# Value projections of two attention branches by seven block products, and weight-block sums made by adding transfers

## The chip, the cores and the metric

The kernel runs on one core of a Trainium2 chip. The metric is the time of one execution on the device in microseconds (us), as a median over runs. The core's engines work side by side: TensorE (PE; its weight loads are listed as PEld), VectorE (DVE), ScalarE (ACT), GpSimd (POOL) and SyncE (SP), which issues the transfers. Each engine takes its instructions in the order of its own queue and waits on semaphores for the others.

## The reference

Two layers of a sequence encoder on an input of 512 rows and 1024 columns, all in float32. A layer projects its input x with one wide weight matrix (1024 x 9216) into the inputs of three branches: retention (four heads, values of 256), chunked attention (eight heads of 64, with a bias by relative position) and differential attention (four heads, each with two softmax maps, values of 128). The branch outputs are projected back to 1024 columns, scaled by sigmoid gates that also come from the projection, added, projected once more, added to x and normalised. A gated feed-forward network (hidden width 2816) and a second normalisation follow. In the core:

```python
h = jnp.einsum('bsd,de->bse', x, w_in[l])
rq, rk, rv, rg, cq, ck, cv, dq, dk, dv, gates = jnp.split(h, splits, axis=-1)
...
p = jax.nn.softmax(s, axis=-1).reshape(B, H, 2, Q_BLOCK, S)
p = p[:, :, 0] - lam * p[:, :, 1]
...
ffn = jnp.einsum('bsf,fd->bsd', jax.nn.silu(u_gate) * u_up, w_ffn_out[l])
```

The parts of `h` that matter here are `cv` and `dv` (512 columns each), the values of chunked and of differential attention, and `rv` and `rg` (1024 columns each), the values and the gate of retention.

## The kernel before

Every float32 operand of a matmul is carried as a pair of float32r tiles, a rounded part and the rest, so that one product of tiles is three matmuls (`mm3`, L121): high by high, high by low, low by high. Weights come from memory in 1 MB pieces into staging tiles `st` (NSTAGE = 3 of them, L49). ScalarE copies the high part into `wh`, VectorE subtracts to make `wl`. There are AHEAD = 3 buffers of each (L48). The work is a list of items (`run_items`, L485): an item is a set of weight pieces and a function that runs its matmuls; the pieces are requested up to three ahead. Between items, and at places within them, small pieces of work (`s_q`, `s_r1`, `s_c1`, `s_d0` and so on) are put in groups beside an item, so that TensorE has matmuls while VectorE and ScalarE do a softmax or a split. A planner lays out each engine's instructions, by the order of the program and the free buffers. Intermediate tiles of 128 x 512 share one pool of 61 slots (NSLOT, L47); gate tiles that are made early (EARLY, L45) are sent to memory and fetched back.

Some products of 512 x 1024 by 1024 x 1024 are not made from eight block products but from seven, with sums of blocks before and after (the Winograd form). `Halves` (L158) holds the weight side: blocks (0,0), (0,1), (1,0), (1,1) of 512 x 512, and four sums T1 to T4 of them. `Quarters` (L228) holds the activation side, whose sums `s_q` makes. `product` (L268) runs one of the seven, with 2 x 4 x 3 = 24 matmuls of 512 columns. This form is used for two groups of retention values and gates in each layer (`u_rvg`, L656: p and q) and for two groups of the output matrix of the feed-forward network (`fout_items`, L1149). VectorE makes the sums T1 to T4 in the staging tiles: `add` (L182), in two instructions each. One staging tile of its own, `sa`, carries (0,0), T1 and T2 through the group. `Staged` (L216) splits a block in two halves.

`cv` and `dv` are projected in the ordinary way by `u_vhl` (L776): for each of four row tiles 8 x 3 matmuls of 512 columns, 96 in all, with the split halves left in slots for the attention that follows. The item of `cv` carries the retention of heads 2 and 3 (`s_r1`, `s_r2`) beside it, the item of `dv` the last steps of chunked attention.

The order of the items is written out from L1021. In the stage before attention it is: first item, gate (0,1), p's m1, gate (0,2), p's y and x, gate (0,3), p's m2 and v, gate (2,0), p's g and h, an item of retention queries (`u_rqk`), q's m1, an item of retention keys, q's y, gate (2,1), q's x, m2, v, g, h, then `cv`. A gate or `u_rqk` item has 48 matmuls of 512 columns.

Of the kernel before, what the change touches and what calls it, by code (L numbers as in the profile page):

```python
# [17 lines left out]
P = 128  # L18
# [26 lines left out]
EARLY = [(0, 0), (0, 1), (0, 2), (0, 3), (2, 0), (2, 1)]  # L45
# [3 lines left out]
NSTAGE = 3  # L49
# [7 lines left out]
def trunk(ctx, tc, x_in, xT_in, w_in, ret_norm_g, da_norm_g, lq1, lk1, lq2, lk2, w_a, w_b, w_c, b_merge, w_out,  # L57
# [12 lines left out]
    make_identity(nc, ident)  # L70
    mhalf = cpool.tile([P, 4], F32, name="mhalf")
    nc.gpsimd.memset(mhalf, -0.5)
    saved = [dram.tile([S, D], F32, name=f"saved{i}") for i in range(2 * DEPTH - 1)]

# [83 lines left out]
    class Halves:  # L158
# [6 lines left out]
        def __init__(self, w, r0, kh, cols=(0, 512)):  # L165
            self.w, self.r0, self.kh, self.cols = w, r0, kh, cols

        def load(self, i, j, tag="st", **kw):
            t = wst.tile([P, 2048], F32, tag=tag, name=tag, **kw)[:, :512 * self.kh]
            t = t.rearrange("p (k c) -> p k c", k=self.kh)  # L170
            r = P * (self.r0 + i * self.kh)
            c = self.cols[j]
            nc.sync.dma_start(t, self.w[r:r + P * self.kh, c:c + 512].rearrange("(k p) c -> p k c", p=P))
            return t

        def parts(self):
            h = max(self.kh // 2, 1)
            return [slice(a, min(a + h, self.kh)) for a in range(0, self.kh, h)]

        def add(self, t, u):  # L180
            for s in self.parts():
                nc.vector.tensor_add(t[:, s], t[:, s], u[:, s])  # L182

        def block(self, t):
            return Staged(t, self.kh, self.parts())

        def b11(self):
            self.a = self.load(0, 0, "sa", bufs=1)
            return self.block(self.a)

        def t1(self):
            self.add(self.a, self.load(0, 1))
            return self.block(self.a)

        def t2(self):
            self.add(self.a, self.load(1, 1))
            return self.block(self.a)

        def b21(self):
            return self.block(self.load(1, 0))  # L200

        def b22(self):
            self.d = self.load(1, 1)
            return self.block(self.d)

        def t3(self):
            c = self.load(0, 1)
            self.add(c, self.__dict__.pop("d"))
            return self.block(c)

        def t4(self):
            b = self.load(1, 0)
            self.add(b, self.__dict__.pop("a"))
            return self.block(b)

    class Staged:  # L216


        def __init__(self, st, nk, parts):
            n = 512 * nk  # L220
            self.nk = nk
            self.hi = wsp.tile([P, 2048], F32R, tag="wh", name="wh")[:, :n].rearrange("p (k c) -> p k c", k=nk)
            self.lo = wsp.tile([P, 2048], F32R, tag="wl", name="wl")[:, :n].rearrange("p (k c) -> p k c", k=nk)
            for s in parts:
                nc.scalar.copy(self.hi[:, s], st[:, s])  # L225
                nc.vector.tensor_sub(self.lo[:, s], st[:, s], f(self.hi[:, s]))  # L226
# [167 lines left out]
    class Norm:  # L394
# [11 lines left out]
        def finish(self, t):  # L406
# [3 lines left out]
            rs = small.tile([P, 2], F32, tag="rs", name="rs")  # L410
            nc.vector.tensor_scalar_add(rs[:, 0:1], mv[:, 1:2], LN_EPS)  # L411
            nc.gpsimd.tensor_tensor(rs[:, 1:2], rs[:, 0:1], mhalf[:, 0:1], op=ALU.pow)
            for z, gam in zip(self.z[t], self.gam):
                nc.vector.scalar_tensor_tensor(z, z, mv[:, 0:1], gam, op0=ALU.subtract, op1=ALU.mult)  # L414
            for hf, (z, bet) in enumerate(zip(self.z[t], self.bet)):
                nc.vector.scalar_tensor_tensor(z, z, rs[:, 1:2], bet, op0=ALU.mult, op1=ALU.add)  # L416
                nc.sync.dma_start(self.dst[P * t:P * t + P, 512 * hf:512 * hf + 512], z)

        def normalise(self, t):
            mv = small.tile([P, 2], F32, tag="mv", name="mv")  # L420
            nc.vector.bn_aggr(mv, self.st[t])
            rs = small.tile([P, 2], F32, tag="rs", name="rs")
            nc.vector.tensor_scalar_add(rs[:, 0:1], mv[:, 1:2], LN_EPS)
# [887 lines left out]
```

## Time and profile before

| What | Value |
|---|---|
| Time, median of 3 runs | 1924.13 us (1923.47 to 1924.18) |
| The profiled execution | 1923.79 us |
| Its span, first to last instruction | 1922.0 us |
| Mean granted TensorE clock | 0.998 |
| Busy: PE, DVE, ACT, POOL | 99%, 68%, 46%, 2% |
| Matmuls | 9250 |
| Moved by DMA | 241 MB, mean 125 GB/s |
| Transfers issued by | SP alone (hardware queue 1: 239.5 MB, 39.2% of the 16 engines' time) |

The span is the profiled execution between its first and last instruction. Busy shares are unions of instruction times; they say how much an engine does, not whether something waits for it. Part 2 of the profile's page cuts the span into 40 slices of 48 us, in tenths.

### The profile page before, as it was taken

The page shows a single profiled execution, that of the slowest core. Times are in us where ns is not written, and L with a number is a line of the kernel's source. Part 1 is how long each engine was busy: PE and PEld are TensorE (multiplying, and loading weights), DVE is VectorE, ACT ScalarE, POOL GpSimd, SP SyncE. Part 2 cuts the span into 40 slices and gives each one's busy share as a digit, 9 for nine tenths or more (in the row PEclk, how much of TensorE's full clock was granted, in tenths as well). Part 3 has the DMA queues.
Part 4 walks back from the last instruction along what each step waited for, and adds up shares of the span by engine and source line. Part 5 has one row for each costly group of instructions (what it writes and reads, how often), then busy time and mean ns, then how long its engine had stood idle before and what let it go on. Part 6 is the DMA issues. An engine that isn't in the chain of part 4 may idle for free. (4 is left out here: it accounts for less than half of the span.)

```text
span 1922.0 us, 23998 instructions
## 1 busy us (share of the span) xinstructions
PE 1907.8 (99%) x9250; PEld 1606.2 (84%) x9250; DVE 1305.7 (68%) x2183; ACT 876.8 (46%) x1551; POOL 46.2 (2%) x73
## 2 busy tenths in 40 slices
PE   9999999999999999999999999999999999999998
PEld 7888888888888888888898888888888898888886
DVE  7677766667765757666588776665776667675666
ACT  5444455567634333333255544554765343333331
POOL 0000000000000000000000000000000000000000
PEclk9999999999999999999999999999999999999999
DMA  7453343233154444434335444332221624444331
GB/s 251 168 171 121 121 135 112 57 94 97 44 183 125 148 137 127 137 109 143 121 140 185 156 138 135 113 95 92 77 87 62 202 78 153 148 137 132 110 127 48
DMA packets 242070, 241.05 MB, mean 125 GB/s; under 512 B 8366, under 2 KB 180516, under 8 KB 241956
## 3 DMA queue, kind: packets, MB, share of 16 engines
q1 hardware_dynamic: 241956, 239.52, 39.2%
q8 instruction: 72, 1.18, 0.3%
q14 instruction: 42, 0.34, 0.1%
HBM read 224.77 MB, written 14.73 MB: 125 GB/s over the span
## 5 line engine op out<-in xcount | busy, mean ns | idle before, releaser
L122 PE MATMUL pt<-xTh,wh 128*128 128x512 f32 (+1 forms) x1584 | 596.8, 377 | 1.5 <-ACT xTh L519 1.5
L123 PE MATMUL pt<-xTl,wh 128*128 128x512 f32 (+1 forms) x1584 | 593.6, 375 | 1.1 <-DVE xTl L520 1.1
L124 PE MATMUL pt<-xTh,wl 128*128 128x512 f32 (+1 forms) x1584 | 593.2, 375 | 0.0
L151 ACT CAST wh<-st 128x1024 fp32r<-128x1024 f32 (+1 forms) x282 | 268.6, 981 | 272.3 <-issue 138.8
L152 DVE TENSOR_TENSOR wl<-st,wh 128x1024 fp32r<-128x1024 f32 (+1 forms) x282 | 314.0, 1137 | 106.8 <-ACT wh L151 106.3
L123 PEld LDWEIGHTS pt<-xTl,wh 128*128 128x128 f32 x1584 | 298.8, 189 | 54.0 <-DVE xTl L520 2.1
L122 PEld LDWEIGHTS pt<-xTh,wh 128*128 128x128 f32 x1584 | 298.3, 189 | 54.4 <-ACT xTh L519 2.3
L124 PEld LDWEIGHTS pt<-xTh,wl 128*128 128x128 f32 x1584 | 298.4, 188 | 53.6
L225 ACT CAST wh<-st 128x1024 fp32r<-128x1024 f32 x64 | 64.9, 1051 | 97.6 <-PE pt L123 65.0
L1105 DVE TENSOR_TENSOR fth<-fth,pt 128x512 f32<-128x512 f32 x44 | 30.2, 686 | 104.4 <-PE pt L124 104.4
L225 ACT CAST wh<-sa 128x1024 fp32r<-128x1024 f32 x48 | 49.6, 1051 | 67.2 <-PE pt L123 64.0
L226 DVE TENSOR_TENSOR wl<-st,wh 128x1024 fp32r<-128x1024 f32 x64 | 76.6, 1221 | 5.3 <-ACT wh L225 5.1
L1103 ACT ACTIVATE fth<-pt 128x512 f32<-128x512 f32 x44 | 26.2, 596 | 107.7 <-PE pt L124 107.7
L313 ACT COPY sw<-pt 32x512 f32<-32x512 f32 (+1 forms) x96 | 55.6, 580 | 33.5 <-PE pt L124 26.5
L226 DVE TENSOR_TENSOR wl<-sa,wh 128x1024 fp32r<-128x1024 f32 x48 | 57.9, 1220 | 18.2 <-ACT wh L225 18.1
L1104 DVE SCALAR_TENSOR_TENSOR fth<-fth,pt 128x512 f32<-128x512 f32 x44 | 30.1, 685 | 58.0 <-ACT fth L1103 58.0
L365 ACT ACTIVATE cE<-cE,mx 128x512 f32<-128x512 f32 (+1 forms) x64 | 35.3, 553 | 38.7 <-DVE mx L363 38.4
L122 PE MATMUL pt<-oah,wh 128*128 128x512 f32 x128 | 51.2, 400 | 0.0
L122 PE MATMUL pn<-wh,xTh 128*128 128x512 f32 x128 | 50.4, 394 | 0.0
L123 PE MATMUL pt<-oal,wh 128*128 128x512 f32 x128 | 50.1, 392 | 0.2
L124 PE MATMUL pt<-oah,wl 128*128 128x512 f32 x128 | 50.0, 391 | 0.0
L122 PE MATMUL pf<-wh,s12h 128*128 128x512 f32 x128 | 50.0, 390 | 0.0
(280 smaller groups left out, 3484.8 us busy)
## 6 DMA issues: line engine op xcount, KB each, us to landing
st<-in_w_in SPq DMA_DIRECT2D x63, 1024.0 KB
st<-in_w_ffn_in SPq DMA_DIRECT2D x88, 512.0 KB
st<-in_w_ffn_out SPq DMA_DIRECT2D x28, 1024.0 KB
st<-in_w_in SPq DMA_DIRECT2D x32, 512.0 KB
th<-th SPq DMA_DIRECT2D x48, 256.0 KB
st<-in_w_branch_a SPq DMA_DIRECT2D x8, 1024.0 KB
st<-in_w_out SPq DMA_DIRECT2D x8, 1024.0 KB
saved<-z SPq DMA_DIRECT2D x24, 256.0 KB
```

Of the source, the lines that this page charges most:

```text
L122: nc.tensor.matmul(ps, lh, rh, start=start, stop=False)
L123: nc.tensor.matmul(ps, lh, rl, start=False, stop=False)
L124: nc.tensor.matmul(ps, ll, rh, start=False, stop=stop)
L151: done = [nc.scalar.copy(self.hi[:, a:b], st[:, a:b]), nc.vector.tensor_sub(self.lo[:, a:b], st[:, a:b], f(self.hi[:, a:b]))]
L152: nc.vector.tensor_sub(self.lo[:, a:b], st[:, a:b], f(self.hi[:, a:b]))]
L225: nc.scalar.copy(self.hi[:, s], st[:, s])
L226: nc.vector.tensor_sub(self.lo[:, s], st[:, s], f(self.hi[:, s]))
L313: nc.scalar.copy(sw[half * b:half * b + half], ps[half * o:half * o + half])
L365: nc.scalar.activation(e, e, AF.Exp, bias=m, scale=-1.0, accum_out=sums[:, nt:nt + 1])
L1103: nc.scalar.activation(t, pg, AF.Tanh, scale=0.5)
L1104: nc.vector.scalar_tensor_tensor(t, t, 1.0, pg, op0=ALU.add, op1=ALU.mult)
L1105: nc.vector.tensor_mul(t, t, pu)
```

## The change

`cv` and `dv` together, 512 x 1024 by 1024 x 1024, become a third group w in each layer, of the same seven products as p and q; `u_vhl` is gone, and `u_rvg` is now a function `u_two` of two column ranges and two functions that take the results. The results of w are split and stored to memory (`v_away`) and fetched back into slots before they are needed (`v_back`).

In `Halves` the sums are no longer made by VectorE. A transfer issued by GpSimd adds the next block to the staging tile (`accum_op=ALU.add`): `more`. A tile starts with a plain load and takes up to three such additions; each waits until the block that stood there before is split. A second tile `c` is begun early (`ahead`). There are two ways through the sums: in the feed-forward network one tile goes (0,0), T1, T2, T4 (`chain=True`) and c is T3; for w, p and q one tile is (0,0), T1, and c goes T3, T2, T4. The order of the seven products is now m1, m2, g, y, x, v, h for w, p and q; it stays m1, y, x, m2, v, g, h in the feed-forward network. `Staged` splits a whole block with one instruction per engine. There is no `sa` tile, and NSTAGE is 4.

The order of the items changes with it: w and p come one after the other before the retention items, with gate (0,2) inside w and no gate inside p; gates (2,0) and (2,1) follow q; gate (0,3) stands before the last output item of the retention branch and is no longer stored. In differential attention the softmax maps are combined without dividing each by its sum: the second is scaled by the ratio of the sums and lambda, and the common factor goes into the normalisation that follows, with the small constant scaled alike.

```diff
-EARLY = [(0, 0), (0, 1), (0, 2), (0, 3), (2, 0), (2, 1)]
+EARLY = [(0, 0), (0, 1), (0, 2), (2, 0), (2, 1)]
-NSTAGE = 3
+NSTAGE = 4
...
-        def add(self, t, u):
-            for s in self.parts():
-                nc.vector.tensor_add(t[:, s], t[:, s], u[:, s])
...
+        def more(self, t, i, j):
+            nc.gpsimd.dma_start(t, self.src(i, j), accum_op=ALU.add)
+
+        def ahead(self):
+            self.c = self.load(0, 1)
+            self.more(self.c, 1, 1)
+
+        def take(self, name, i=None, j=None):
+            t = self.__dict__[name]
+            b = Staged(t, self.kh)
+            if i is None:
+                del self.__dict__[name]
+            else:
+                self.more(t, i, j)
+            return b
+
+        def m1(self):
+            self.a = self.load(0, 0)
+            return self.take("a", 0, 1)
...
+        def y(self):
+            return self.take("a", *((1, 1) if self.chain else ()))
+
+        def x(self):
+            return self.take("a" if self.chain else "c", 1, 0)
+
+        def g(self):
+            return self.take("c", *(() if self.chain else (0, 0)))
+
+        def h(self):
+            return self.take("a" if self.chain else "c")
...
-            for s in parts:
-                nc.scalar.copy(self.hi[:, s], st[:, s])
-                nc.vector.tensor_sub(self.lo[:, s], st[:, s], f(self.hi[:, s]))
+            nc.scalar.copy(self.hi, st)
+            nc.vector.tensor_sub(self.lo, st, f(self.hi))
...
-            rs = small.tile([P, 2], F32, tag="rs", name="rs")
+            rs = small.tile([P, 1], F32, tag="rs", name="rs")
...
-        def u_rvg(hp):
+        def u_two(left, right, left_done, right_done):
...
             def x(j, ps):
-                u, y = g(name="tu"), t["y", j]
+                u, y, c = t.pop(("m", j)), t["y", j], t.pop(("g", j))
                 t["u", j] = u
-                nc.vector.tensor_sub(u, ps, t["m", j])
+                nc.vector.tensor_sub(u, ps, u)
                 nc.vector.tensor_add(y, y, u)
+                nc.vector.tensor_add(u, u, c)
+                nc.vector.tensor_add(c, c, y)
+                right_done(2 + j, c)
...
-        def u_vhl(dst, base, wd):
...
+        def v_away(dst, wd):
+            def done(t, c):
+                for hf in range(2):
+                    s = g(F32R, "vhl")
...
+                    dst[t, hf] = dram.tile([P, 512], F32, name=f"v{l}_{wd}_{t}_{hf}")
+                    nc.sync.dma_start(dst[t, hf], f(s))
+            return done
+
+        def v_back(dst):
+            def fn():
+                for k, away in list(dst.items()):
+                    dst[k] = g(F32R, "vhl")
+                    nc.sync.dma_start(f(dst[k]), away)
+            return fn
...
         def s_d1(h):
...
-                    nc.vector.tensor_scalar_mul(E[1][pk][:, cs], E[1][pk][:, cs], R[1][:, nt:nt + 1])
-                    nc.vector.scalar_tensor_tensor(E[0][pk][:, cs], E[0][pk][:, cs], R[0][:, nt:nt + 1],
-                                                   E[1][pk][:, cs], op0=ALU.mult, op1=ALU.add)
+                    nc.vector.scalar_tensor_tensor(E0[pk][:, cs], E1[pk][:, cs], R[:, nt:nt + 1], E0[pk][:, cs],
+                                                   op0=ALU.mult, op1=ALU.add)
...
+        w, p, q = u_two(CV, DV, v_away(cv, 64), v_away(dv, 128)), u_rvg(0), u_rvg(1)
+            (u_first(),), (u_gate(0, 1), [w["ahead"], s_q(0)], [s_q(1)]), (w["m1"], [], [s_q(2)]), (w["m2"], [], [s_q(3)]),
+            (u_gate(0, 2),), (w["g"],), (w["y"], [], [s_r1(0)]), (w["x"], [p["ahead"]]), (w["v"], [], [s_r1(1)]), (w["h"],),
+            (p["m1"],), (p["m2"],), (p["g"],), (p["y"],), (p["x"], [q["ahead"]]), (p["v"],), (p["h"],),
+            (u_rqk(rq, RQ, 1), [], [s_r2(0)]), (q["m1"],), (u_rqk(rk, RK, 1), [s_r2(1)], [s_r3(0)]), (q["m2"], [], [s_r3(1)]),
+            (q["g"],), (q["y"],), (q["x"],), (q["v"],), (q["h"],),
+            (u_gate(2, 0), [s_r1(2)], [s_r1(3)]), (u_gate(2, 1), [s_r2(2)], [s_r2(3)]),
+            (u_cqk(0), [s_r3(2)], [s_r3(3), v_back(cv)]),
...
+            (u_branch(0, 2), *c(4)), (u_cqk(3), *c(5)), (u_gate(0, 3), *c(6)), (u_branch(0, 3), *c(7)),
+            (u_dqk(0), *c(8)), (u_gate(1, 0), [s_c3(7), v_back(dv)], d(0)[1]), (u_branch(1, 0), *d(1)), (u_dqk(1),),
...
-            hv = Halves(w_ffn_out[l], r0, kh)
+            hv = Halves(w_ffn_out[l], r0, kh, chain=True)
...
+        outs = [fout_items(gi) for gi in range(len(GROUPS))]
...
+            for n, it in enumerate(outs[gi][1]):
+                item(*it, [outs[gi][0]] if n == 1 else [])
```

More of the change, by code (lines that the diff above doesn't have):

```diff
@@ L180, in add @@
-        def add(self, t, u):
-            for s in self.parts():
[L182 to L214, printed above, removed]
+            nc.sync.dma_start(t, self.src(i, j))
```

131 lines of the change are left out of this document (54 added, 77 removed).

## The prediction

> **What bounds the kernel now.** I read the profile's summary first, then who waits for whom on TensorE, then stretches of the span, then single instructions of the stages that the change touches.
>
> The summary, parts 1 and 2:
>
> ```profile
> span 1922.0 us, 23998 instructions
> PE 1907.8 (99%) x9250; PEld 1606.2 (84%) x9250; DVE 1305.7 (68%) x2183; ACT 876.8 (46%) x1551; POOL 46.2 (2%) x73
> ...
> PE   9999999999999999999999999999999999999998
> ...
> DVE  7677766667765757666588776665776667675666
> ...
> DMA  7453343233154444434335444332221624444331
> ```
>
> TensorE is busy in every slice. A busy TensorE need not be at its peak, so the waits of TensorE decide; this is the whole list:
>
> ```profile
> PE pt L122 <- ACT xTh L519: 1.5, 2, 1.2
> PE warm L507 <- POOL ident masks.py:199: 1.5, 1, 1.5
> PE pt L123 <- DVE xTl L520: 1.1, 2, 0.8
> PE pco L854 <- DVE cPl L112: 0.7, 2, 0.3
> PE px L435 <- DVE z L426: 0.5, 2, 0.3
> ```
>
> It adds up to 5.3 us in 1922, mostly at the start. So a matmul that is left out is worth its whole place in the row, and every new wait of TensorE is paid in full. No other engine has anything to give. The price of one matmul comes from a stretch with nothing but products of `product` (L268): m2, v, g, h of the last group, 4 x 24 = 96 matmuls (the row counts two more, cut by its ends). Columns: length, busy time and count of PE, PEld, DVE, ACT, POOL, granted clock, DMA share, GB/s.
>
> ```profile
> 187.20:209.00 21.80, 21.80 (x98) 18.06 (x97) 19.49 (x25) 11.26 (x14) 0.00 (x0) 1.00 0.69 222
> ```
>
> 21.80 / 96 = 0.227 us per 512-column matmul, at granted clock 1.00, and 24 x 0.227 = 5.45 us per product. (The 389 ns that the groups give for one is its way through the array, not its place in the row.)
>
> **The change part by part.**
>
> *Matmuls.* The two `u_vhl` items of a layer are these rows (tile `pn`):
>
> ```profile
> L122 PE MATMUL pn<-wh,xTh x128: 389/389/477, 208.9 to 1334.4; 128*128 128x512 f32 x128
> ...
> L123 PE MATMUL pn<-wl,xTh x128: 389/389/398, 209.1 to 1334.7; 128*128 128x512 f32 x128
> ...
> L124 PE MATMUL pn<-wh,xTl x128: 389/389/398, 209.4 to 1334.9; 128*128 128x512 f32 x128
> ```
>
> Removed: 3 x 128 = 384. Added: 2 layers x 7 products x 24 = 336. 48 fewer x 0.227 = **10.9 us less**. That is all the change can gain.
>
> *Adds.* `Halves.add` (L182) goes:
>
> ```profile
> L182 DVE TENSOR_TENSOR sa<-sa,st x32: 1215/1219/1224, 41.9 to 1783.6; 128x1024 f32<-128x1024 f32 x32
> ...
> L182 DVE TENSOR_TENSOR st<-st x16: 1218/1220/1228, 88.0 to 1831.5; 128x1024 f32<-128x1024 f32 x16
> L182 DVE TENSOR_TENSOR st<-st,sa x16: 1216/1220/1227, 96.8 to 1842.6; 128x1024 f32<-128x1024 f32 x16
> ```
>
> 64 x 1.22 = 78 us of VectorE. No wait of TensorE ends in L182, so this gives 0 by itself. In exchange 5 groups x 4 x 2 layers = 40 adding transfers of 1 MB are issued on POOL. Nothing like them is in the trace, and they are the unknown that decides.
>
> *What an adding transfer delays.* A block is split by ScalarE, then VectorE, when one of the three `wh`/`wl` buffers (AHEAD, L48) is free, that is, when the product three places earlier has ended. Waits and one such block, then the VectorE half of another:
>
> ```profile
> ACT wh L225 <- PE pt L123: 129.0, 30, 7.6
> ```
> ```profile
> 83.92 2.00 ACT L225 CAST wh<-st 128x1024 fp32r<-128x1024 f32 x2 [2.16 <-PE pf L124]
> ```
> ```profile
> 188.69 2.35 DVE L226 TENSOR_TENSOR wl<-st,wh 128x1024 fp32r<-128x1024 f32 x2
> ```
>
> The new `Staged` works on whole blocks: 2.00 + 2.35 = 4.35 us one after the other, where halves took 1.05 + 2.35 = 3.4. Between back-to-back products the lead is 2 x 5.45 = 10.9, so the 0.95 more costs 0 while the block is there in time. For a sum it may not be: the next sum in the same buffer may start only when the one before is split. The tightest place is the second group of the new order, p, with no gate between its seven products. Block g gets its buffer when w's h ends; then split g, transfer, split x, transfer, split h, and h is wanted after m1, m2, g, y, x, v = 6 x 5.45 = 32.7 us. With L from issue to landing and q for what stands ahead in the queues of ScalarE and VectorE,
>
> late = 3 x 4.35 + 2 L + 3 q - 32.7 = 2 L + 3 q - 19.65 per layer.
>
> For q I take 0.5: VectorE is at 19.49 / 21.80 = 89% in the stretch above, its commonest other instruction there is 0.69 us, and a full 2.35 is the worst. The other places have more room: w has a gate, q an `u_rqk` item (10.9 each) within the same chain, which moves the limit on L up by at least 2.7; in the FFN a 10.9 us item follows each product, so a sum has 16.35 - 4.35 = 12 us and the lead besides.
>
> *L.* Lower end: a plain load of the same 1 MB, here the issue and the instruction that waited for its landing:
>
> ```profile
> 175.42 0.37 SPq L173 DMA_DIRECT2D st<-in_w_in  x1
> ```
> ```profile
> 180.85 2.36 DVE L182 TENSOR_TENSOR st<-st,sa 128x1024 f32<-128x1024 f32 x2 [4.79 <-DMA st<-in_w_in]
> ```
> ```profile
> 84.00:87.60 3.60, 3.60 (x18) 2.98 (x17) 3.57 (x4) 1.92 (x2) 0.00 (x0) 1.00 0.90 291
> ```
>
> 5.4 us in all, 3.6 of it the transfer (291 GB/s x 3.6 us = 1.05 MB). Upper end: source read, destination read and sum written as three such transfers in turn, 16.2. Between them I take a second pass of the bytes over the same 16 engines, 3.6, and for POOL's own work 1.0, as its longest ordinary instructions have:
>
> ```profile
> L750 POOL TENSOR_TENSOR rsr<-ss,mhalf 128x4 f32<-128x4 f32 x8 | 9.9, 1239 | 430.3 <-DVE ss L749 430.3
> ...
> L941 POOL TENSOR_TENSOR rsr<-ss,mhalf 128x4 f32<-128x4 f32 x8 | 8.1, 1008 | 267.6 <-DVE ss L940 267.6
> ```
>
> L = 5.4 + 3.6 + 1.0 = 10.0, late = 20.0 + 1.5 - 19.65 = 1.85 per layer, **3.7 us** in two.
>
> The plain load's row would have the sum cost nothing more than a copy. The Trainium skill speaks against that ("Collectives: The Full Stack", Part 3, the bandwidth ceiling): an add in the transfer engines needs two source reads, and its rate was about half that of a copy. By the row alone the forecast would be the full gain, by the rule a transfer of 2 x 3.6 and L = 9.0, which would just fit; no run here shows an adding transfer yet.
>
> *Queues.* POOL's queue gets the 40 transfers, each waiting for a split or a landing. Behind them stand only L750's powers of `s_r2`(0) and (1), beside q; VectorE's `ro` (L756) and the transposes of `s_r3` wait for those, with more than one 5.45 us product between. I cost this at 0, and at what exceeds 5.45 otherwise. SP's queue gets per layer 16 stores of 256 KB (`v_away`), later 16 loads (`v_back`), and loses two gate stores and loads. Stores of the kind hold it now:
>
> ```profile
> SPq L969 <- ACT th L965: 67.3, 20, 7.2
> ```
>
> 3.4 us each; weight loads queue behind. A load must be out 5.4 + 4.35 = 9.75 us ahead, and four buffers less the two that hold sums still let two wait, two products or more: 0, or the excess over that if the cover goes.
>
> *Moves.* Retention (`s_r1`, `s_r2` of heads 2, 3) lay under `u_vhl`, 96 matmuls or 21.8 us, and now lies under two gates, 96 matmuls too. `s_c3`, `s_c1` of the last heads lose the second `u_vhl` and get one 10.9 us item per step, as the heads before them, where VectorE is at 61% and TensorE never waits long:
>
> ```profile
> 240.00:290.00 50.00, 49.87 (x249) 41.58 (x249) 30.54 (x64) 25.21 (x52) 3.09 (x5) 1.00 0.46 143
> ```
>
> 0. The shorter `s_d1`, the one-column `rs` and the moved allocation save VectorE's time only: 0.
>
> *Sum.* The profiled execution took 1923.8 (span 1922.0 and 1.8 around it): 1923.8 - 10.9 + 3.7 = 1916.6. The median of the three runs, 1924.13, is 0.3 above it: **1917** in its terms.
>
> **The rivals.** What a measurement of this kernel can tell from no change is about 0.2%, 3.85 us: below 1920.3 or above 1928.0.
>
> 1. *Everything hides.* L up to 9.1 makes late zero: 1924.1 - 10.9 = 1913.2. For it: the q group's five products now run back to back with no wait. Against: those loads need no second read.
>
> 2. *Slower: the chain through the two sums of p.* Two layers cost 2 x (2 L - 18.15) = 4 L - 36.3. From L = 11.8 it eats the gain, from 12.8 the kernel is slower by over 0.2%, at 14 it stands at 1924.1 - 10.9 + 19.7 = 1933, at the upper end 16.2 at 1942. For it: each us of L counts four times (two sums, two layers), and POOL's work for 512 rows of 2 KB may exceed 1.0. Against: DMA is at 0.69 there at most, so there is room.
>
> 3. *No change: transfers meet each other.* q's first sum is started beside p's x (`q["ahead"]`), just when p's last sum is moving; its plain load adds 3.6 to that one: 2 x 3.6 = 7.2, 1924.1 - 10.9 + 3.7 + 7.2 = 1924. Or POOL is held up by VectorE, once by a 2.35 us split for each of the four transfers: 9.4, 1926. The Trainium skill ("SBUF — State Buffer", "Who interferes with whom") has the two share a port pair, with the later one blocked; it also says that two-input instructions take only its read side, and those rows are what VectorE runs here, so I give this little. The trace has no transfer from POOL to test it.
>
> 4. *It does not do what it says.* The number of matmuls is fixed by the loops, so 48 fewer is sure; only the waits are open.
>
> **How the numbers follow.** Forecast (L 9.1 to 10.8, so 1913.2 to 1920.3, middle 1917): 0.38. Rival 1: 0.18. Rival 3 and L up to 12.8: 0.17. Rival 2: 0.27. Faster 0.38 + 0.18 = 0.56, same 0.17, slower 0.27. The range goes from 1912, the full gain and a microsecond, to L = 14.5, 4 x 14.5 - 36.3 = 21.7, so 1935; some 0.1 of rival 2 lies above, little below.
>
> **What would show it.** The count of 512-column matmuls falls by 48 and each stays at 0.227 apart. Waits of TensorE for `wh`/`wl` at the start of p's h, about 1.9 us twice, show the chain; none there, with all else alike, is rival 1; over 5 us is rival 2. A last landing 10 us after POOL's issue fits L; under 7 or over 13 says that a term of L was wrong. If L750's powers or the `v_away` stores are what TensorE's waits lead back to, the queues were mis-costed. If new waits lie in the FFN or in the attention, the picture of one tight place was wrong.

## The result, and the profile after

The changed kernel takes **1972.42 us** (1971.51 to 1977.8) against 1923.80 of the kernel before (median of four runs): a ratio of 1.026, 95% interval 1.0241 to 1.0279. It is slower by 48.6 us, where 1917 with a range to 1935 was predicted. The profiled execution took 1977.8 us, 5.4 above the median, with a span of 1975.9. Parts 1 and 2 of its page:

```profile
span 1975.9 us, 24017 instructions
...
PE 1917.2 (97%) x9202; PEld 1606.1 (81%) x9202; DVE 1250.7 (63%) x2065; ACT 890.6 (45%) x1513; POOL 96.7 (5%) x113
...
PE   9988999999999999999998989999999999999998
...
PEclk9999999999999999999998999999999999999999
DMA  8776544332145465463457855432321454656441
```

The 48 matmuls are gone (9250 to 9202). TensorE has holes in slices 3 and 4 and again in 22 and 24, where the first stage of each layer lies, the three groups w, p and q. The same stretch of that stage in both layers, columns as in the prediction (length, busy time and count of PE, PEld, DVE, ACT, POOL, granted clock, DMA share, GB/s), first before, then after:

```profile
80.00:150.00 70.00, 70.00 (x328) 58.73 (x327) 52.54 (x67) 32.47 (x51) 1.03 (x1) 1.00 0.47 155
1060.00:1150.00 90.00, 90.00 (x435) 75.91 (x434) 66.45 (x85) 43.72 (x71) 2.93 (x2) 1.00 0.42 142
```
```profile
80.00:150.00 70.00, 58.35 (x245) 46.64 (x244) 40.32 (x52) 30.29 (x40) 6.44 (x5) 0.95 0.79 209
1060.00:1150.00 90.00, 74.86 (x312) 60.12 (x311) 52.41 (x67) 39.42 (x50) 6.44 (x5) 0.91 0.75 202
```

Of 763 matmuls that were started in these 160 us before, 557 are left. VectorE and ScalarE do less too: nobody is full, so everyone waits for something. The waits of TensorE, longest groups first (us in total, times, longest):

```profile
PE pf L122 <- ACT wh L227: 9.8, 2, 4.9
PE pf L123 <- DVE wl L228: 9.3, 6, 1.8
PE pco L857 <- ACT cPh L106: 6.3, 3, 3.0
PE pf L122 <- ACT s43h L106: 6.1, 1, 6.1
PE pf L122 <- DVE tm L684: 4.3, 2, 2.9
PE psr L122 <- DVE tm L684: 3.4, 1, 3.4
```

Only the first two are what the prediction looked for, a product that waits for its weights. The others wait for activations (`s43h`), for a bank that VectorE has not emptied (`tm`), and, in the attention, for `cPh`. All groups together make 49.6 us, against 5.3 before. That falls short of the loss, which is 48.6 us and the 10.9 that the 48 matmuls should have saved: some of it is TensorE at half clock. One such stretch, and the same times in the kernel before:

```profile
107.80:114.40 6.60, 5.58 (x17) 4.39 (x16) 6.57 (x15) 4.95 (x7) 0.00 (x0) 0.50 0.41 152
```
```profile
107.80:114.40 6.60, 6.60 (x30) 5.46 (x30) 5.10 (x7) 3.70 (x5) 0.00 (x0) 1.00 0.63 177
```

Over the whole execution:

```profile
core 0: 1975.9 us, clock 0.988
```

Against 0.998 before: about 0.012 x 1975.9 / 0.5 = 47 us ran at 0.50, where it was 0.002 x 1922.0 / 0.5 = 8. Half of the 39 us between them, some 20 us, is the most that this can have cost. The waits and the clock together cover the loss.

**Where the waits come from.** The adding transfers as POOL issues them; x2 is two in one row:

```profile
70.92 2.59 POOL L180 DMA_DIRECT2D st<-in_w_in  x2 [28.78 <-DVE s12l L112]
...
133.41 2.59 POOL L180 DMA_DIRECT2D st<-in_w_in  x2 [15.00 <-DVE wl L228]
146.37 1.28 POOL L180 DMA_DIRECT2D st<-in_w_in  x1 [10.37 <-DVE wl L228]
```

The first of the pair at 70.92 is p's sum ahead, wanted much later; the second, issued at about 71.7, is w's sum for x, wanted next. And q's sum ahead is the second of the pair at 133.41, before p's last sum at 146.37. The casts of ScalarE that wait for w's and p's sums, with the idle time before each in brackets:

```profile
88.26 1.90 ACT L227 CAST wh<-st 128x2048 fp32r<-128x2048 f32 x1 [9.23 <-DMA st<-in_w_in]
...
102.02 1.91 ACT L227 CAST wh<-st 128x2048 fp32r<-128x2048 f32 x1 [7.54 <-DMA st<-in_w_in]
...
160.00 1.90 ACT L227 CAST wh<-st 128x2048 fp32r<-128x2048 f32 x1 [10.13 <-DMA st<-in_w_in]
```

From 71.7 to 88.3 is 16.6 us, from 146.4 to 160.0 is 13.6; w's last sum, which meets no other, takes 92.8 to 102.0, 9.2 us. For w the queue explains it: p's sum ahead was still 7.5 us from landing when w's was issued behind it. For p it explains little: q's sum ahead landed 2.3 us after p's last one was issued, and two other sums of this kernel that had 2.2 and 3.4 us ahead of them in the queue landed in 8.4 and 8.5 us. What else was late there shows in the share of the transfer engines from issue to landing (the last but one figure) of these three sums:

```profile
71.70:88.30 16.60, 16.59 (x72) 13.10 (x72) 7.21 (x13) 3.30 (x8) 1.81 (x2) 1.00 1.01 231
146.00:160.00 14.00, 10.95 (x47) 8.75 (x47) 4.68 (x6) 2.63 (x6) 1.28 (x1) 1.00 1.07 294
92.80:102.00 9.20, 9.20 (x42) 7.57 (x42) 2.29 (x1) 1.68 (x3) 1.26 (x1) 1.00 0.84 183
```

The two late ones moved with the engines full (1 is full), w's beside p's sum and SP's transfers, p's beside SP's: 294 GB/s for 14 us are 4.1 MB, of which p's sum is 1.05. The theory below names the queue alone; the experiments change the order and the company of a sum together and do not part the two.

While the cast waits, nothing behind it in ScalarE's queue runs, and VectorE stands at the subtraction behind the cast. Both groups over the whole kernel:

```profile
ACT wh L227 <- DMA st<-in_w_in: 59.4, 9, 10.2
```
```profile
DVE wl L228 <- ACT wh L227: 122.3, 51, 11.3
```

Everything else that the two engines owe TensorE (`s43h`, `tm`, the decay products of the retention) comes late by that. At 130 us one more late thing shows, a decay table, and why (SP's queue):

```profile
130.22 0.69 DVE L720 TENSOR_TENSOR rtmp<-psr,dh 128x512 f32<-128x512 f32 x1 [6.41 <-DMA dh<-in_decay]
```
```profile
113.48 7.73 SPq L785 DMA_DIRECT2D v<-vhl  x6
121.26 1.55 SPq L708 DMA_DIRECT2D dh<-in_decay  x1
```

The load `dh` stands behind six stores of `v_away`, which wait for VectorE (SP's stores of `vhl` wait 32.9 us for it in the whole kernel). So the theory for the experiments, T: sums that meet in POOL's queue and land late make ScalarE and VectorE stand, and TensorE loses by their other work as much as by the block itself. The rivals: A, the chain of two sums is too long even alone; B, the stores and the order of the attention are the loss; C, VectorE is the bound; D, an adding transfer costs wherever it is.

### The profile page after: what moved, and what is told of

The parts are those of the page before. It is cut to its first block, busy times and chain, and to the rows that moved or that the text cites. A ratio compares the mean times of both kernels' runs of the same rounds, so it can differ in the third digit from the quotient of the medians.

```text
span 1975.9 us, 24017 instructions
## 1 busy us (share of the span) xinstructions
PE 1917.2 (97%) x9202; PEld 1606.1 (81%) x9202; DVE 1250.7 (63%) x2065; ACT 890.6 (45%) x1513; POOL 96.7 (5%) x113
## 3 DMA queue, kind: packets, MB, share of 16 engines
q1 hardware_dynamic: 237348, 229.04, 36.0%
q0 software_dynamic: 21120, 41.95, 12.2%
## 5 line engine op out<-in xcount | busy, mean ns | idle before, releaser
L152 DVE TENSOR_TENSOR wl<-st,wh 128x1024 fp32r<-128x1024 f32 (+1 forms) x266 | 295.1, 1132 | 111.2 <-ACT wh L151 107.0
L228 DVE TENSOR_TENSOR wl<-st,wh 128x2048 fp32r<-128x2048 f32 x70 | 160.3, 2290 | 122.3 <-ACT wh L227 122.3
L227 ACT CAST wh<-st 128x2048 fp32r<-128x2048 f32 x70 | 133.6, 1909 | 198.2 <-PE pt L123 90.4
L122 PE MATMUL pf<-wh,s43h 128*128 128x512 f32 x160 | 64.0, 400 | 12.0 <-ACT s43h L106 6.1
L122 PE MATMUL pf<-wh,xTh 128*128 128x512 f32 x144 | 58.8, 408 | 9.8 <-ACT wh L227 9.8
L123 PE MATMUL pf<-wl,s12h 128*128 128x512 f32 x160 | 63.3, 396 | 4.3 <-DVE wl L228 4.3
L123 PE MATMUL pf<-wl,s43h 128*128 128x512 f32 x160 | 63.6, 398 | 1.6 <-DVE wl L228 1.6
L124 PE MATMUL pf<-wh,s43l 128*128 128x512 f32 x160 | 63.6, 398 | 0.8 <-DVE s43l L112 0.8
L124 PE MATMUL pf<-wh,s12l 128*128 128x512 f32 x160 | 62.8, 393 | 0.0
L123 PE MATMUL pf<-wl,xTh 128*128 128x512 f32 x144 | 58.5, 406 | 3.4 <-DVE wl L228 3.4
```

What stands on the lines that cost most here:

```text
L122: nc.tensor.matmul(ps, lh, rh, start=start, stop=False)
L123: nc.tensor.matmul(ps, lh, rl, start=False, stop=False)
L124: nc.tensor.matmul(ps, ll, rh, start=False, stop=stop)
L152: nc.vector.tensor_sub(self.lo[:, a:b], st[:, a:b], f(self.hi[:, a:b]))]
L227: nc.scalar.copy(self.hi, st)
L228: nc.vector.tensor_sub(self.lo, st, f(self.hi))
```

## The experiments

Times are medians; the kernel before stood at 1922.77 to 1923.84 in the same series.

**The sums in the order of the program**

```diff
-            nc.gpsimd.dma_start(t, self.src(i, j), accum_op=ALU.add)
+            tc.keep_in_program_order(nc.gpsimd.dma_start(t, self.src(i, j), accum_op=ALU.add))
```

> Edit: the changed kernel, with its adding transfers kept in the order of the program, so that the sum that p (or q) orders beside w's (or p's) last sum no longer goes ahead of it in POOL's queue. Theory T (transfers that meet in one queue land 13.6 to 16.5 us after issue instead of 8.4, ScalarE's and VectorE's queues then stand behind the late block, and TensorE stalls and is given half clock): w's second sum and p's last one land within 9 to 10 us, the stalls at 102-110, 160-166 and 1138-1145 us shrink, and the kernel gives back 15 to 35 us: 1937 to 1957. Rival A (the chain of two sums is too long even at 8.4 us): 1965 to 1972. Rival B (the stores of the values and the attention's order are the loss, not the sums): 1968 to 1974.

1959.23 us: 13.2 back, just under T's 15 and outside its range. POOL and the cast for p's last sum:

```profile
141.54 2.60 POOL L180 DMA_DIRECT2D st<-in_w_in  x2 [12.39 <-DVE wl L228]
```
```profile
150.64 1.91 ACT L227 CAST wh<-st 128x2048 fp32r<-128x2048 f32 x1 [5.59 <-DMA st<-in_w_in]
```

The last sum is now the first of the pair and there after 9.1 us instead of 13.6. So meeting is real, but it is only a quarter of the loss; A and B both still stand.

**The sums by VectorE**

```diff
-            nc.gpsimd.dma_start(t, self.src(i, j), accum_op=ALU.add)
+            u = self.load(i, j)
+            for s in (slice(0, 2), slice(2, 4)):
+                nc.vector.tensor_add(t[:, s], t[:, s], u[:, s])
```

> Edit: the changed kernel, each adding transfer replaced by a plain load of the second block and two VectorE additions (the order of products, the third group of seven, the split of whole blocks and everything else stay). Theory T: the waits of ScalarE's casts for a sum go, what is left is VectorE, 6 sums of about 2 x 1.2 us more in each group; most of the 52 us that the two w/p/q stretches lost come back: 1925 to 1945. Rival B (stores and attention's order are the loss): 1968 to 1976. Rival C (VectorE is the bound of these stretches in itself, and the additions by transfer were its cover): slower than the changed kernel, 1985 or more.

1931.18 us: 41.2 back, with the stores, the order of the products and the whole-block splits as in the changed kernel. B as the main loss and C are out. The second block is loaded early into a buffer of its own here, so a sum needs no transfer after its buffer is free: VectorE's additions wait 4.1 us for blocks in the whole kernel.

**Adding transfers in the feed-forward network alone** (kernel before; `Adding` is the new `Halves` with its whole-block splits)

```diff
-            hv = Halves(w_ffn_out[l], r0, kh)
+            hv = Adding(w_ffn_out[l], r0, kh, chain=True)
...
-NSTAGE = 3
+NSTAGE = 4
```

> Edit: the kernel before, with adding transfers in place of loads and VectorE additions in the feed-forward network alone (its two groups of seven products in each layer), and a fourth staging buffer. Theory T: here sums never meet in the queue and are 20 us apart, the trace of the changed kernel has them landing in 8.5 us and no new stall of TensorE in this stage: no difference, 1921 to 1927. Rival D (adding transfers cost wherever they are, by traffic or by POOL): 2 to 8 us slower.

1922.80 us, ratio 1.000 (0.999 to 1.001). D is out. That sums never meet here is not so: in each layer one was issued about 1 us behind another and landed after 13.6 and 13.5 us. So a late sum is not by itself a loss. The page's issues of this kernel give the usual time of a sum:

```profile
st<-in_w_ffn_out POOLq DMA_DIRECT2D x16, 1024.0 KB, 8.6
```

**The last value product of the chunk attention later**

```diff
-(u_gate(1, 0), [s_c3(7), v_back(dv)], d(0)[1])
+(u_gate(1, 0), [v_back(dv)], [s_c3(7)] + d(0)[1])
```

> Edit: the changed kernel, with the last head's value product of the chunk attention put behind the second half of the gate product (1, 0) instead of behind its first half. If the split of that head's weights, standing behind the rotary of the differential keys on ScalarE, is what costs TensorE 2.95 us of waiting and one stretch at half clock in each layer (about 4.9 us), the kernel is 8 to 10 us faster than the changed one: 1962 to 1965, and the rows PE pco L857 <- ACT cPh leave the list of waits. If the wait only moves to the next product, 1970 to 1973.

1968.92 us: 3.5 back by medians, less than the 8 to 10 expected. The spans of the profiled executions differ by 8.1 (1975.9 to 1967.8), but that of the changed kernel was a slow one, 5.4 above its median. The rows for `cPh` are gone from the waits. In the changed kernel the cast stood behind these on ScalarE:

```profile
421.82 2.53 ACT L106 CAST ks<-rot 64x512 fp32r<-64x512 f32 x4 [2.01 <-DVE rot L319]
424.37 1.07 ACT L106 CAST cPh<-ptr 128x512 fp32r<-128x512 f32 x2
```

**The decay tables early** (on the first experiment's kernel)

```diff
-            (u_gate(0, 2),), (w["g"],), ...
+            (u_gate(0, 2), [early_dh]), (w["g"],), ...
...
+        def early_dh():
+            dhs.update({h: s_dh(h) for h in range(2)})
...
```

(`s_dh` loads one table; `s_r1` takes the table that is there already.)

> Edit: the changed kernel with the sums in program order, and the decay tables of heads 0 and 1 are loaded beside the gate product (0, 2), before the first value store, instead of at the score product that needs them. If the stores of the values ahead of the decay load in SP's queue are part of the loss (trace of the changed kernel: VectorE waits 6.41 us for dh, TensorE then 1.6 us twice, and a stretch at half clock), 4 to 10 us come back against the order experiment's 1959.23: 1949 to 1955, and the stalls of psr for rtmp and of p's first product for rtmp leave the list. If the decay load was only what happened to be waited for last while VectorE stood behind w's sums, 1957 to 1961.

1949.87 us, 9.4 back. The stores ahead of one load of 256 KB were a cause of their own.

**Room for p's last sum** (on the one before)

```diff
-(p["x"], [q["ahead"]]), (p["v"],)
+(p["x"], [q["ahead"]]), (u_gate(2, 0),), (p["v"],)
...
-(u_gate(2, 0), [s_r1(2)], [s_r1(3)]), (u_gate(2, 1), [s_r2(2)], [s_r2(3)]),
-(u_cqk(0), [s_r3(2)], [s_r3(3), v_back(cv)]),
+(u_gate(2, 1), [s_r1(2)], [s_r1(3)]),
+(u_cqk(0), [s_r2(2), s_r2(3)], [s_r3(2), s_r3(3), v_back(cv)]),
```

> Edit: as the one before, and the gate product (2, 0), 10.9 us of TensorE that needs no sum, is moved from behind q to between p's x and p's v, with the score and value work of heads 2 and 3 that it carried put on the two items behind q. Theory T: p's last sum has then 10.9 us more, so the waits of p's h for wh and wl go (1.83 + 0.35 and 1.82 us of waiting and one half-clock stretch by the order experiment's trace) and 4 to 7 us come back: 1943 to 1950. If the chain is not the cause there, no difference from the one before it; if the work of heads 2 and 3 on the fewer items behind q stands in the way instead, 3 or more us slower than the one before it.

1948.82 us, no difference. TensorE's waits for `wh`, first without, then with the gate:

```profile
PE pf L122 <- ACT wh L227: 2.5, 3, 1.8
```
```profile
PE pf L122 <- ACT wh L227: 6.0, 2, 3.9
```

The waits at p's h did go, as T said, but p's x, two products earlier, now waits up to 3.9 us where it was 1.8. Room at the place that the prediction named is worth nothing by itself; why p's x got later is not settled.

**VectorE's sums and the late value product**

On the kernel with VectorE's sums:

```diff
-(u_gate(1, 0), [s_c3(7), v_back(dv)], d(0)[1])
+(u_gate(1, 0), [v_back(dv)], [s_c3(7)] + d(0)[1])
```

> Edit: the changed kernel with both repairs that are known so far, VectorE additions in place of the adding transfers, and the last head's value product behind the gate product's second half. The vector experiment's 1931.18 less 8 to 10 us if the attention's stall of 2.95 us and its half-clock stretch in each layer go without a new one: 1921 to 1924, so level with the kernel before although it does 48 products of 512 columns fewer (10.9 us): the rest then stands in the w/p stretch of layer 1 (4.01 us and a half-clock stretch).

1921.43 us, ratio 0.999 (0.998 to 0.9999): as expected. VectorE has no gap in this stretch of layer 1 (length, busy time and count of VectorE, clock, DMA share, GB/s), so that C, no bound of the whole, is one there:

```profile
1045.00:1069.00 24.00, 24.00 (x34) 0.86 0.68 226
```

**Mixed: only sums with room by transfer**

```diff
-                self.more(t, i, j)
+                (self.more if self.chain or name == "a" else self.add)(t, i, j)
```

> Edit: as the one before, but the two sums of each group that have room (the one ordered ahead, and the one behind m1 that has two products before its use) and those of the feed-forward network are adding transfers again; only the two sums that follow each other in one buffer (for x and for h) are VectorE additions. Theory T (a sum by transfer is harmless where it has room and meets no other): as the one before or up to 6 us faster, since VectorE is freed of 6 of 12 sums per layer there: 1915 to 1924. Rival D (an adding transfer costs by standing in ScalarE's queue wherever a w/p/q block is made by one): 1928 or more.

1926.53 us, between the two expectations. With the decay tables early:

```diff
-            (u_gate(0, 2),), (w["g"],), ...
+            (u_gate(0, 2), [early_dh]), (w["g"],), ...
```

> Edit: the mixed kernel (1926.53: the sums with room by transfer, the two that follow each other by VectorE, the last head's value product late) with the decay tables of heads 0 and 1 loaded early. Its trace has 2.00 and 1.64 us of waiting at 123-126 us behind rtmp of layer 0 and a half-clock stretch there, all of it beside the decay load: if that is what sets the mixed kernel behind the vector kernel, 1919 to 1922. If the sums by transfer themselves hold it up (1.45 us at 79.9 for s43h, nothing removed), 1925 to 1928.

1918.97 us, ratio 0.9976 (0.9967 to 0.9986), faster than the kernel before and than the one with VectorE's sums (1921.43). A transfer that has two products' time costs nothing that shows.

**VectorE's sums, decay tables early, head 1's scores one group later**

```diff
-(w["v"], [], [s_r1(1)]), (w["h"],), (p["m1"],)
+(w["v"],), (w["h"],), (p["m1"], [], [s_r1(1)])
```

> Edit: the vector kernel (1921.43) with the decay tables loaded early, and the score product of head 1 moved from w's v to p's m1, because in layer 1 VectorE works without a gap from 1041 to 1069 us with that head's decay products among w's sums, and TensorE waits 4.00 us for ty at its end. If that crowding is the last loss of the stage (4.0 us and two half-clock stretches of 3.4 us that cost half of their length), 1914 to 1918. If the same work only crowds VectorE later, 1920 to 1923.

1921.83 us, no gain. The 4.0 us wait is gone, and another of 2.9 us for `th` stands at 1043: the work only crowds elsewhere.

**The whole-block split alone, on the kernel before**

```diff
-            for s in parts:
-                nc.scalar.copy(self.hi[:, s], st[:, s])
-                nc.vector.tensor_sub(self.lo[:, s], st[:, s], f(self.hi[:, s]))
+            nc.scalar.copy(self.hi, st)
+            nc.vector.tensor_sub(self.lo, st, f(self.hi))
```

> Edit: the kernel before, with the blocks of the products of seven split whole (one copy and one subtraction of 2048 columns instead of two of 1024 each) and nothing else. The prediction costed this at nothing, since the blocks are split ahead of their products: 1921 to 1926. If the split's longer way (4.35 instead of 3.4 us) lies on the path wherever a sum comes just before its product, 3 to 10 us slower.

1923.42 us, ratio 1.0001 (0.9992 to 1.001): nothing, as predicted.

**The sums by halves** (on the kernel with program order and early decay)

```diff
-            tc.keep_in_program_order(nc.gpsimd.dma_start(t, self.src(i, j), accum_op=ALU.add))
+            for s in (slice(0, 2), slice(2, 4)):
+                tc.keep_in_program_order(nc.gpsimd.dma_start(t[:, s], self.src(i, j)[:, s], accum_op=ALU.add))
...
-            nc.scalar.copy(self.hi, st)
-            nc.vector.tensor_sub(self.lo, st, f(self.hi))
+            for s in (slice(0, 2), slice(2, 4)):
+                nc.scalar.copy(self.hi[:, s], st[:, s])
+                nc.vector.tensor_sub(self.lo[:, s], st[:, s], f(self.hi[:, s]))
```

> Edit: the kernel with sums in program order and decay loads early (1949.87), each adding transfer as two of half a block, and the blocks split by halves again, so that the first half can be split while the second lands. If most of a sum's 8.4 to 13 us is bytes, the first half lands some 3 to 4 us earlier and the chain of a sum is 3 to 4 us shorter: 1938 to 1945. If it is a fixed latency and POOL's own time of 1.28 us for each, the two land as late as the one or later: 1949 to 1960.

1924.22 us: 25.7 back, far more than the 5 to 12 expected. The chain of p's last two sums, POOL and then ScalarE, first with whole blocks:

```profile
120.04 1.28 POOL L180 DMA_DIRECT2D st<-in_w_in  x1 [10.32 <-ACT tm L673]
137.36 2.59 POOL L180 DMA_DIRECT2D st<-in_w_in  x2 [16.04 <-DVE wl L228]
```
```profile
132.84 1.90 ACT L227 CAST wh<-st 128x2048 fp32r<-128x2048 f32 x1 [9.78 <-PE pf L123]
...
146.34 1.91 ACT L227 CAST wh<-st 128x2048 fp32r<-128x2048 f32 x1 [7.33 <-DMA st<-in_w_in]
```

and by halves:

```profile
119.39 2.44 POOL L181 DMA_DIRECT2D st<-in_w_in  x2 [11.07 <-ACT wh L229]
130.32 1.20 POOL L181 DMA_DIRECT2D st<-in_w_in  x1 [8.48 <-DVE wl L230]
133.78 3.68 POOL L181 DMA_DIRECT2D st<-in_w_in  x3 [2.25 <-DVE wl L230]
```
```profile
127.70 1.05 ACT L229 CAST wh<-st 128x1024 fp32r<-128x1024 f32 x1 [4.19 <-DMA st<-in_w_in]
131.16 1.05 ACT L229 CAST wh<-st 128x1024 fp32r<-128x1024 f32 x1 [2.41 <-DMA st<-in_w_in]
...
136.44 1.08 ACT L229 CAST wh<-st 128x1024 fp32r<-128x1024 f32 x1
139.83 1.05 ACT L229 CAST wh<-st 128x1024 fp32r<-128x1024 f32 x1 [2.31 <-DMA st<-in_w_in]
```

The first half of the last sum is issued at 130.32, before the second half of the sum ahead of it is there to be cast (131.16). From the first issue to the last sum's first cast it is 17.1 us instead of 26.3, to its second 20.4. Of the 26.3 the first whole sum took 12.7 us to land, though only 0.6 us stood before it in POOL's queue, with the engines' share at 1.08 until then; the second took 8.9, at 0.82. ScalarE now stands 28.0 us for sums, VectorE 47.1 behind it:

```profile
ACT wh L229 <- DMA st<-in_w_in: 28.0, 12, 4.2
```
```profile
DVE wl L230 <- ACT wh L229: 47.1, 55, 4.0
```

Yet the transfer engines are fuller than ever in 80 to 150 us, and TensorE almost without a gap:

```profile
80.00:150.00 70.00, 69.16 (x310) 56.94 (x310) 51.80 (x75) 36.91 (x56) 14.61 (x12) 1.00 0.99 259
```

So over the stretch it was not bandwidth that the changed kernel lacked (0.79 in its row above); but while its late sums were moving the engines were full (1.01 and 1.07), and a sum in a chain pays for that moment.

**Splits by halves, sums whole** (on the same kernel as the half sums)

```diff
-            nc.scalar.copy(self.hi, st)
-            nc.vector.tensor_sub(self.lo, st, f(self.hi))
+            for s in (slice(0, 2), slice(2, 4)):
+                nc.scalar.copy(self.hi[:, s], st[:, s])
+                nc.vector.tensor_sub(self.lo[:, s], st[:, s], f(self.hi[:, s]))
```

> Edit: the kernel with sums in program order and decay loads early (1949.87), its blocks split by halves, each sum still one transfer of a whole block. If the gain of the half sums (25.6 us) came from the transfers (a half is released, refilled and landed while the other half is still being split), this gives back at most 5 us: 1944 to 1950. If it came from the shorter split (first products start on the first half, 1.9 us less of standing for each block), 1924 to 1935.

1950.53 us against 1949.87: nothing. The 25.7 us need the transfers by halves; a shorter split alone gives none of it. Whether half transfers with whole splits would do was not run.

**Half sums and half splits on the changed kernel, nothing else**

```diff
-            nc.gpsimd.dma_start(t, self.src(i, j), accum_op=ALU.add)
+            for s in (slice(0, 2), slice(2, 4)):
+                nc.gpsimd.dma_start(t[:, s], self.src(i, j)[:, s], accum_op=ALU.add)
...
-            nc.scalar.copy(self.hi, st)
-            nc.vector.tensor_sub(self.lo, st, f(self.hi))
+            for s in (slice(0, 2), slice(2, 4)):
+                nc.scalar.copy(self.hi[:, s], st[:, s])
+                nc.vector.tensor_sub(self.lo[:, s], st[:, s], f(self.hi[:, s]))
```

> Edit: the changed kernel with each adding transfer as two of half a block and blocks split by halves; order of the sums, decay loads and attention as in the changed kernel. If meeting sums and the late decay load are causes of their own, the 22 us that they gave remain lost: 1940 to 1950. If they only weigh because the blocks are late by a few us (half sums take the slack back), 1923 to 1932.

1942.90 us: 29.5 back. Order and decay tables together are then worth 18.7 (1942.90 to 1924.22), against 22.6 with whole blocks: causes of their own, nearly additive.

**Half sums, program order, early decay, late value product**

On the half-sums kernel:

```diff
-(u_gate(1, 0), [s_c3(7), v_back(dv)], d(0)[1])
+(u_gate(1, 0), [v_back(dv)], [s_c3(7)] + d(0)[1])
```

> Edit: the half-sums kernel (1924.22), with the last head's value product behind the second half of the gate product (1, 0). Its trace has the attention's 2.95 us in each layer and no other wait over 1.3 us but the start's; without half-clock stretches there, so less comes back than the changed kernel's 8 us: 1916 to 1919, faster than the kernel before by 0.25 to 0.4%.

**1916.62 us**, ratio 0.9961 (0.9949 to 0.9974): faster than the kernel before by 7.2 us. No group of TensorE's waits is above 1.5 us, and the first ones are those of the start:

```profile
PE warm L511 <- POOL ident masks.py:199: 1.5, 1, 1.5
PE pt L122 <- ACT xTh L523: 1.2, 1, 1.2
```

**The mixed kernel, its transfers by halves**

On the mixed kernel with early decay tables:

```diff
-            nc.gpsimd.dma_start(t, self.src(i, j), accum_op=ALU.add)
+            for s in (slice(0, 2), slice(2, 4)):
+                nc.gpsimd.dma_start(t[:, s], self.src(i, j)[:, s], accum_op=ALU.add)
...
-            nc.scalar.copy(self.hi, st)
-            nc.vector.tensor_sub(self.lo, st, f(self.hi))
+            for s in (slice(0, 2), slice(2, 4)):
+                nc.scalar.copy(self.hi[:, s], st[:, s])
+                nc.vector.tensor_sub(self.lo[:, s], st[:, s], f(self.hi[:, s]))
```

> Edit: the mixed kernel with early decay loads (1918.97), its sums by transfer by halves and blocks split by halves. Its trace has one wait of 3.59 us behind the split of s43 at 81 us and 6.8 us of half clock, while ScalarE and VectorE stood behind w's first sums: if half sums take that too, 1912 to 1916, near the whole 10.9 us; if not, 1917 to 1920.

1917.27 us, ratio 0.9966 (0.9953 to 0.9978), not to be told from the one before. Expected was less; one wait of 2.7 us for `s43h` stays. The reason given for that wait does not hold either: in the mixed kernel with early decay tables VectorE has no gap over 0.2 us from 61 to 83 us, so it is full there and does not stand behind a sum.

**The loss in one line.** 1972.42 less 13.2 (order in POOL's queue), 9.4 (decay load in SP's queue), 25.7 (sums by halves) and 7.6 (value product) is 1916.6. Each term is a difference of two medians and holds, by the spread of the runs, to some 2 us; in another order of the edits the terms come out differently (halves first: 29.5, then 18.7 for the order and the decay load); 1923.8 - 10.9 = 1912.9 would be the whole gain, so 3.7 is left unexplained. Of the rivals, A is right in part: with the sums in order, the transfers by halves still bring 25.7, the largest term.

## Why the prediction was wrong, point by point

- **Matmuls, 10.9 us less: right.** 48 fewer, and products run at 5.45 us each where nothing waits (from one matmul's start to the next the median is 227 ns before and after).
- **Adds, 0: not contradicted, and not tested apart.** Back on VectorE the sums cost 41.2 us less than the transfers that replaced them, but they also leave VectorE without a gap in one stretch of layer 1.
- **L = 10.0: too long for a sum alone, too short for those that decide.** With nothing before it in POOL's queue a sum of the changed kernel lands in 8.3 to 10.7, POOL's own part 1.28 where 1.0 was taken; the late ones, behind another sum or beside SP's transfers, take 13.6 to 16.6. The step "a second pass of the bytes" held: from the page of the changed kernel,

```profile
q1 hardware_dynamic: 237348, 229.04, 36.0%
q0 software_dynamic: 21120, 41.95, 12.2%
```

an adding megabyte takes 12.2 / 41.95 = 0.291% of the engines' time, a plain one of SP's queue 36.0 / 229.04 = 0.157%: the ratio is 1.85. The Trainium skill's half rate ("Collectives: The Full Stack", Part 3) agrees with that. The L of 9.0 that the prediction worked out by that rule was nearer than its own 10.0 to the medians of the changed kernel's profile, 9.2 for w, p and q and 8.5 in the feed-forward network; but by it the whole gain would have been kept, which is further from the time measured.
- **One tight place, 1.85 us per layer: the step that failed.** p's h waited 4.9 us for `wh` in each layer (the 9.8 in the first row of the waits) and 1.8 and 1.5 us for `wl`, 13 in all; that is 6.7 and 6.4 per layer, over the 5 that the prediction named as the sign of its rival 2. The formula with the two landings as measured (8.4 and 13.6, so 2L = 22.0) gives 3.8 per layer, so the chain was sized too low; yet those 13 us are a part of 48.6 + 10.9 = 59.5 us of loss. The sentence "the other places have more room" counted products only. It left out that a late block stops ScalarE's and VectorE's queues, at every sum and not only at the tightest; q was put at 0.5 us for what stands ahead in the queues, and nothing for what stands behind. The room given to p's h left p's x with a longer wait and gained nothing.
- **Whole-block split, 0: right as a split, wrong in what it holds.** Alone it costs nothing, before (1.0001) and with whole sums (1950.53). But the prediction took the chain's split and L as fixed lengths in a row; by halves they overlap, which is worth 25.7 to 29.5 us, the largest term.
- **Queues, 0: wrong, 13.2 and 9.4 us.** For POOL only L750's powers were looked for behind a sum, not another sum; rival 3 had the meeting of q's sum ahead with p's last one, at 7.2, without the same at w. For SP the weight loads were reckoned with, and the decay load, wanted in the middle of w, was not.
- **Moves, 0: wrong, 7.6 us** (3.5 and 9.8 on two other kernels). VectorE's 61% was the argument; the wait was for ScalarE, whose queue had the rotary keys of the next head in front.
- **Feed-forward network, no wait: right** (1.000).
- **Half clock: not in the sum at all**; up to some 20 us of the loss.
- **Rival 2** had the side and the right word, chain, but needed L of 14 everywhere to reach 1933 and of 16.2 to reach 1942; the time outside the range came from what late blocks and loads held up in the three queues, the clock's part in it not separated. Its argument against itself, that the engines are at 0.69 at most, did not hold where it counted: they stood at 1.01 and 1.07 while the late sums moved.

## What to carry to other kernels

When a block's preparation becomes a transfer into the same buffer, price it by what its late arrival stops: everything behind its first reader in that engine's queue, and what each of those owes others. Chain such transfers by pieces, so that one piece is refilled while the next is still being read. Before a queue is costed at nothing, list what is issued in it around the tight place in the order in which it will really be issued, the small loads too. Look at the transfer engines' share while the piece in the chain is moving, and not at the mean of the stage.

## What the runs showed of the hardware

- Transfers of POOL's queue land in the order of issue: in all 13 kernels with such transfers none overtook another, and a sum with 7 us or more of another before it took 12.4 to 16.5 us in the changed kernel, against 8.3 to 10.7 with none. The Trainium skill ("DMA: Bandwidth & Descriptors", "SWDGE vs HWDGE vs iDMA") states that only one such queue is allocated; the traces agree, their pages show q0 alone for it.
- Other traffic lengthens such a transfer too: 12.7 us at an engine share of 1.08 with 0.6 us of another sum before it, 8.9 at 0.82 (the kernel with program order and early decay).
- 1 MB pieces were the slower choice. The Trainium skill ("DMA: Bandwidth & Descriptors", "Bandwidth") advises batches of 1 MiB or more for the rate. Here halves of 512 KB nearly kept the rate (engine time 12.9% for the same 41.95 MB against 12.5% beforehand) and brought 25.7 us, through the buffers.
- TensorE's clock fell to 0.50 for 3.4 us or a multiple after a single wait of 3.0 us (the attention's for `cPh`, in the changed kernel) and after one of 2.1 us (for `ty` at 107 us, in the kernel with early decay). Yet the same wait of 3.0 us stands in both layers of the half-sums kernel, and no such stretch follows. The Trainium skill ("TensorE: Matmul & The Clock Gate", Part 1) gives an idle window of about 3.4 us, free-running, as the condition; the lengths of the stretches agree, the waits were shorter, and their length alone does not decide. In the kernel of 1916.62 us, whose waits past the start stay under 1.3 us, the mean clock is 0.998 again. That the clock itself cost the 20 us was not tested apart from the waits.
